# The first stage of a two-layer encoder trunk: constant matmuls ahead of it, another order of its splits, small vectors on GpSimd's queue

## The chip, the cores and the metric

The kernel runs on one core of a Trainium2 chip. The metric is the device time of one execution in microseconds (us). Three executions of the kernel before took 936.38, 937.65 and 938.26 us; their median, 937.65 us, is the time that the change is compared with. Engine names: PE is TensorE (PEld its weight loads), DVE is VectorE, ACT is ScalarE, POOL is GpSimd, SP is SyncE, which here does nothing but issue DMAs.

## What is computed

Two layers of a bidirectional encoder over 256 tokens of width 1024, all in fp32. The part that matters here is the beginning of a layer:

```
h    = rms_norm(x, g_mix)
proj = h @ w_in            # w_in: 1024 x 5792, columns split into
c_q, c_kv, k_r, d_q, d_k, d_v, s_q, s_k, s_v, gate_logits
# latent attention (c_q 256, c_kv 128, k_r 32 wide), differential attention,
# windowed attention, three sigmoid gates; then
x = x + (sum of gate * branch output) @ w_out
x = x + (gelu(conv3(h2 @ w_ffn_gate)) * (h2 @ w_ffn_up)) @ w_ffn_down
x = x + sigmoid(rms_norm(x) @ w_ple_gate) * rms_norm(p @ w_ple_proj)
```

Besides the large weights there are some twenty small vectors per layer (norm gains, convolution taps, lambda vectors, sinks), and the token positions, from which rope tables and distances are made.

## The kernel before

**Products.** Each fp32 matrix product is made as three products of a narrower format (fp32r): both operands are split into a hi part (a copy by ACT that rounds) and a lo part (the rest, a subtraction by DVE), and `mm3` (line 342) adds hi by hi, hi by lo and lo by hi in PSUM. So each weight has to pass through ACT (line 91) and DVE (line 92) before TensorE can use it. `Stream` (line 60) does this for the weights, in units of up to 128 x 1024: `_load` issues the DMA of a unit on SP's queue, `_split` makes the two parts `whi` and `wlo`, and `get` hands the next unit to the product loop after it has loaded four units ahead and split two ahead. There are four buffers each for raw, hi and lo units, so the load of unit 4 waits until unit 0 is split.

**The first stage.** Nothing of the trunk can start before x is transposed and scaled with the gain g_mix. x lies in four tiles (two token tiles t, two column halves h), loaded by `load_x`. `transpose_half` (line 378) takes one half: for each of two pairs kp of 128-column blocks it makes four transposes on TensorE into one PSUM bank, then for each block of the pair a hi part on ACT (line 352) and a lo part on DVE (line 353), scaled with the gain column `gm`. `gm` itself is a transpose of the small tile `mrow`, into which g_mix is loaded. Then `gemm` (line 395) for chunk A (c_q, c_kv, k_r; 416 columns) uses four units of 128 x 832, two blocks of h each: 12 products a unit, 48 in all, into two PSUM banks. `evict_A` copies them out.

**Order.** Lines 560 to 579 stand under a manual schedule: ACT, DVE, SP and PE run what is given there in the order in which it is written. POOL doesn't; its instructions, and everything outside of this block, are ordered by a list scheduler with priorities. In the block, both halves of x are transposed first; unit 0 is split after the first half and unit 1 after the second; then comes the product loop of chunk A, whose first `get` also splits unit 2, and so on. `load_gains(0)` stands in it too: 14 small DMAs on SP's queue into the tile `grows`, behind the first four weight units and ahead of unit 4. `finish_gains` (line 219) transposes `grows` on TensorE (`gT_ps`), behind the last product of chunk A and, in TensorE's order, ahead of the first gate chunk `g00`; the gains in `gT`, the rope tables and the position tables (`positions_setup`, line 269) follow from it at low priority.

**What follows.** The order of the rest of the mixer on TensorE is the string `ORDER` (line 51). The first point at which it needs small results of the first stage is `Tmk0`: transposes of the normalised latent keys `uk0*tok`, which need the statistics `L0st` of chunk A, computed in small steps on POOL (lines 542 to 550, 730, 732).

**Second layer's gains.** `load_gains(1)` is called behind the transposes for the FFN of layer 0 (line 1116). Its tile takes the buffer of `mrow`, and the scheduler put its memset at 3.9 us and its 14 DMAs between 27 and 48 us.

Of the kernel before, what the change touches and what calls it, by code (L numbers as in the profile page):

```python
# [11 lines left out]
F32 = mybir.dt.float32  # L12
# [6 lines left out]
P = 128  # L19
# [15 lines left out]
DEFER_M = 2  # L35
HI = 400
# [10 lines left out]
# The order of a layer's token mixer on the tensor engine, after the latent projections. Chunks of projection columns:  # L47
# g<branch><half> gates, b<branch><half> branch outputs, dq/dk/dv differential, sq/skv windowed q and kv (one word for
# each weight unit); uq/ukv latent expansions; T<x> transposes of x; and the stages of attention (m latent, d
# differential, w windowed): s scores, p transposed probabilities, o values, dt transposed differential output.  # L50
# [9 lines left out]
class Stream:  # L60
    """Weight units in the order of their use: loads run ahead of the splits, splits ahead of the products."""

    def __init__(self, nc, pools, ahead_load, ahead_split):
        self.nc = nc
        self.raw_pool, self.hi_pool, self.lo_pool = pools
        self.al, self.asp = ahead_load, ahead_split
        self.specs = []
        self.raw = {}
        self.split = {}
        self.nl = self.ns = self.nu = 0  # L70
        self.behind = {}  # unit: the instructions its hi and lo parts stay behind
# [46 lines left out]
def kernel(ctx: ExitStack, tc: tile.TileContext, a: dict, out: bass.AP):  # L118
# [37 lines left out]
    nc.sync.dma_start(mrow[0:8, :], a["g_mix"][0].rearrange("(j p) -> j p", p=P))  # L156
# [20 lines left out]
    def load_gains(l):  # L177
        g = {}
        rows = lay.tile([P, P], F32, tag="grows", name=f"grows{l}")
        nc.gpsimd.memset(rows, 1.0)  # L180
        q = nc.sync
        q.dma_start(rows[R_MIX:R_MIX + 8, :], a["g_mix"][l].rearrange("(j p) -> j p", p=P))
        q.dma_start(rows[R_QL:R_QL + 2, :], a["g_q_lora"][l].rearrange("(j p) -> j p", p=P))
        q.dma_start(rows[R_KL:R_KL + 1, :], a["g_kv_lora"][l].rearrange("(j p) -> j p", p=P))
        q.dma_start(rows[R_CW:R_CW + 66, :], a["conv_w"][l].rearrange("t (j p) -> (t j) p", p=P))
        q.dma_start(rows[R_CB:R_CB + 22, :], a["conv_b"][l].rearrange("(j p) -> j p", p=P))
        q.dma_start(rows[R_FFN:R_FFN + 8, :], a["g_ffn"][l].rearrange("(j p) -> j p", p=P))
        q.dma_start(rows[R_PIN:R_PIN + 8, :], a["g_ple_in"][l].rearrange("(j p) -> j p", p=P))
        q.dma_start(rows[R_DO:R_DO + 1, :], a["g_diff_out"][l].rearrange("(j p) -> j p", p=P))
        for r, nm in ((R_DQ, "g_diff_q"), (R_DK, "g_diff_k"), (R_WQ, "g_win_q"), (R_WK, "g_win_k")):  # L190
            q.dma_start(rows[r:r + 1, :].rearrange("j (d p) -> j d p", d=2),
                        a[nm][l].rearrange("(j d p) -> j d p", j=1, d=1).broadcast_to([1, 2, 64]))
        for r, nm in ((R_MQ, "g_mla_q"), (R_MK, "g_mla_k")):
            q.dma_start(rows[r:r + 1, 0:64], a[nm][l, 0:64].rearrange("(j p) -> j p", j=1))
        g["rows"] = rows
        return g
# [72 lines left out]
    def positions_setup():  # L269

# [6 lines left out]
        nc.vector.tensor_copy(pos_col, pos_col_i)  # L277
        pos_row = tmp.tile([P, S], F32, tag="p", name="pos_row")
        nc.vector.tensor_copy(pos_row, pos_row_i)
# [58 lines left out]
    def pin(ins):  # L338
        """Keeps an instruction behind what TensorE has been given so far."""
        order(ins, last_pe[0])  # L340
# [37 lines left out]
    def transpose_half(src, h, hi, lo, gcol, name, scale=None):  # L378
        res = []
        for kp in range(2):  # L380
            b = bank(f"{name}T{h}{kp}")
            bv = b.rearrange("p (a n) -> p a n", a=2)
            for i in range(2):
                c = (kp * 2 + i) * P
                for t in range(NT):
                    TR(bv[:, i, t * P:(t + 1) * P], src[t][h][:, c:c + P], ident)
            k0 = h * 4 + kp * 2
            if gcol is None:
                res.append(split(hi[:, k0:k0 + 2, :], lo[:, k0:k0 + 2, :], bv, scale))
            else:  # L390
                for i in range(2):
                    res.append(split(hi[:, k0 + i, :], lo[:, k0 + i, :], bv[:, i, :], gcol(k0 + i)))
        return res

    def gemm(name, nk, n, lhs, evict, alloc=None):
        accs = [(alloc or accbank)(f"{name}a{t}") for t in range(NT)]
        k = 0
        while k < nk:
# [3 lines left out]
            if k + per == nk:  # L402
                steps = [(i, t) for t in range(NT) for i in range(per)]
            for i, t in steps:
# [77 lines left out]
    def softmax_T(p_t, name):  # L482
        """P [q, (qt, k)] -> its transpose as a hi/lo pair [k, (kt, q)]."""
# [10 lines left out]
    # ================= one layer =================  # L494
    def layer(l):
# [12 lines left out]
        # 0,1: sums of squares; 2: mean square + eps; 3: its rsqrt; 4: half of that; 5: eps * (2)  # L508
# [20 lines left out]
        # 6,7: c_q, c_kv mean squares, +eps/rmix^2; 8: k_r mean square share; 9,10: their rsqrt;  # L529
        # 11: eps term of q heads; 12: k_r and eps term of k heads; 13: factor of k_r  # L530
# [26 lines left out]
        ag = gemm(n_ + "A", KT, 416, hT, evict_A)  # L557
        if l == 0:
            ET = mybir.EngineType
            with tc.manual_schedule(engines={ET.Activation, ET.DVE, ET.SP, ET.PE}):  # L560
# [8 lines left out]
                for h in range(2):  # L569
                    transpose_half(x, h, hTh, hTl, lambda k: gm[:, k:k + 1], n_ + "mix")  # L570
                    W.presplit(1 + h)
                next(ag)
                next(ag)
# [31 lines left out]
        @low  # L605
        def norm_heads(acc, nh, t, name, extra=None):
            """Per-head factor rmix * rsqrt(mean((rmix*q)^2) + eps) [* extra] of the raw projections."""
# [20 lines left out]
        def defer(n, key, fn):  # L628
            """Emits fn behind n more fill units (or before the transposes that need it)."""
            deferred.append([n, key, fn])  # L630
# [9 lines left out]
        def drain(accs, n, view=None, oview=None):  # L640
            """Copies a chunk's raw sums out of PSUM, so that its banks are free at once."""
# [172 lines left out]
        def pair_out(pts, vsel, dst, j, name):  # L814
            """Values of a pair of heads: the columns hold V's hi and lo parts, whose products are summed on the way out."""
# [13 lines left out]
        def scores2(q, k, jq, jk, name):  # L829
            """Scores of two heads held on the two halves of the partitions, one bank for each."""  # L830
# [426 lines left out]
```

## Time and profile before

| | us |
|---|---|
| median of three executions | 937.65 |
| lowest, highest | 936.38, 938.26 |
| span of the profiled execution | 933.5 |
| TensorE busy in it | 915.4 |
| DVE, ACT, POOL busy | 700.9, 604.3, 125.1 |

The profiled execution is known by its span, from its first to its last instruction; the times of whole executions lie 2.9 to 4.8 us above that span, which is what lies around it. A profile row names the engine, the line of the kernel, the operation, the tile written and the tiles read, and in brackets what the engine waited for just before. Rows that start with SPq are DMA issues on SP's queue; their time is that of the issue, not of the transfer. A row with x7 merges seven instructions in a row, and its second number runs from the first one's start to the last one's end. Consecutive matmuls overlap, so the spacing of their starts counts and not the length of one.

### The profile page before, as it was taken

The numbers are of one execution on the slowest core, as the hardware profiler recorded it, in microseconds if no ns is written. First come the engines' busy times: TensorE is split into PE (matmuls) and PEld (weight loads), VectorE is DVE, ScalarE is ACT, GpSimd is POOL, SyncE is SP. The second block draws the span as 40 slices with busy tenths as digits, with TensorE's granted clock in tenths as the row PEclk, the third lists the DMA queues.
The fourth block names the chain that finished last, engine by engine and source line by source line (L and its number), as shares of the span: only waits on it lengthen the run. The fifth ranks groups of instructions, "written<-read, shape, count | busy, mean of one in ns | idle before, by whom it ended". The sixth has DMA issues, their size and how long they took to land.

```text
span 933.5 us, 15007 instructions
## 1 busy us (share of the span) xinstructions
PE 915.4 (98%) x5511; PEld 803.1 (86%) x5511; DVE 700.9 (75%) x1193; ACT 604.3 (65%) x1084; POOL 125.1 (13%) x239
## 2 busy tenths in 40 slices
PE   7999999999999999999999999999999999999997
PEld 6888887788799999999888888787888999999986
DVE  4798789887688667677777887979766767767684
ACT  5878876885565455555676788688655555555472
POOL 2834111010110000000143423010001100000010
PEclk9999999999999999999999999999999999999999
DMA  6755435356646666666556555344465566656642
GB/s 195 223 173 167 140 100 164 108 164 199 185 136 203 188 183 190 185 181 198 151 159 185 160 165 163 111 138 116 143 216 158 177 185 180 196 175 194 193 150 87
DMA packets 101709, 155.97 MB, mean 167 GB/s; under 512 B 7316, under 2 KB 58372, under 8 KB 101636
## 3 DMA queue, kind: packets, MB, share of 16 engines
q1 hardware_dynamic: 101636, 155.02, 55.3%
q8 instruction: 43, 0.70, 0.3%
q14 instruction: 30, 0.25, 0.1%
HBM read 153.95 MB, written 1.05 MB: 166 GB/s over the span
## 4 chain that ended last, share of the span: by engine, by line
PE 87%; POOL 3%; issue 3%; ACT 3%; DVE 2%; DMA 1%; SPq 1%; POOLq 0%; ACTq 0%; DVEq 0%
PE L1u L327 7%; PE L0u L327 7%; PE L0g L327 7%; PE L1g L327 7%; PE L1dn L327 6%; PE L0dn L327 6%; PE L0g20a L327 1%; PE L1g20a L327 1%; PE L1dva L327 1%; PE L0dva L327 1%; PE L1dka L327 1%; PE L0dka L327 1%; PE L1g00a L327 1%; PE L0pg0a L327 1%; PE L1g21a L327 1%
## 5 line engine op out<-in xcount | busy, mean ns | idle before, releaser
L92 DVE TENSOR_TENSOR wlo<-raw,whi 128x1024 fp32r<-128x1024 f32 (+3 forms) x292 | 350.9, 1207 | 144.9 <-ACT whi L91 144.2
L91 ACT ACTIVATE whi<-raw 128x1024 fp32r<-128x1024 f32 (+3 forms) x292 | 304.0, 1045 | 201.9 <-PE L0g L327 28.5
L327 PE MATMUL L0g<-L0fTh,wlo 128*128 128x256 f32 x176 | 49.8, 283 | 0.0
L327 PE MATMUL L0u<-L0fTh,whi 128*128 128x256 f32 x176 | 49.8, 283 | 0.0
L327 PE MATMUL L0u<-L0fTl,whi 128*128 128x256 f32 x176 | 49.8, 283 | 0.0
L327 PE MATMUL L0u<-L0fTh,wlo 128*128 128x256 f32 x176 | 49.8, 283 | 0.0
L327 PE MATMUL L1g<-L1fTh,wlo 128*128 128x256 f32 x176 | 49.8, 283 | 0.0
L327 PE MATMUL L1u<-L1fTh,whi 128*128 128x256 f32 x176 | 49.8, 283 | 0.0
L327 PE MATMUL L1u<-L1fTl,whi 128*128 128x256 f32 x176 | 49.8, 283 | 0.0
L327 PE MATMUL L1u<-L1fTh,wlo 128*128 128x256 f32 x176 | 49.8, 283 | 0.0
L327 PE MATMUL L1g<-L1fTl,whi 128*128 128x256 f32 x176 | 49.8, 283 | 0.0
L327 PE MATMUL L0g<-L0fTl,whi 128*128 128x256 f32 x176 | 49.8, 283 | 0.0
L327 PE MATMUL L0g<-L0fTh,whi 128*128 128x256 f32 x176 | 49.8, 283 | 0.0
L327 PE MATMUL L1g<-L1fTh,whi 128*128 128x256 f32 x176 | 49.8, 283 | 0.0
L327 PEld LDWEIGHTS L0g<-L0fTl,whi 128*128 128x128 f32 x176 | 33.8, 192 | 0.4
L327 PEld LDWEIGHTS L0g<-L0fTh,whi 128*128 128x128 f32 x176 | 33.7, 192 | 0.4
L327 PEld LDWEIGHTS L1g<-L1fTl,whi 128*128 128x128 f32 x176 | 33.7, 192 | 0.4
L327 PEld LDWEIGHTS L1g<-L1fTh,whi 128*128 128x128 f32 x176 | 33.8, 192 | 0.4
L327 PEld LDWEIGHTS L0u<-L0fTh,whi 128*128 128x128 f32 x176 | 33.8, 192 | 0.0
L327 PEld LDWEIGHTS L0u<-L0fTl,whi 128*128 128x128 f32 x176 | 33.8, 192 | 0.0
L327 PEld LDWEIGHTS L0u<-L0fTh,wlo 128*128 128x128 f32 x176 | 33.8, 192 | 0.0
L327 PEld LDWEIGHTS L1u<-L1fTh,whi 128*128 128x128 f32 x176 | 33.8, 192 | 0.0
(1732 smaller groups left out, 2653.8 us busy)
## 6 DMA issues: line engine op xcount, KB each, us to landing
raw<-in_w_in_dram SPq DMA_DIRECT2D x84, 512.0 KB
raw<-in_w_ffn_gate_dram SPq DMA_DIRECT2D x44, 512.0 KB
raw<-in_w_ffn_up_dram SPq DMA_DIRECT2D x44, 512.0 KB
raw<-in_w_ffn_down_dram SPq DMA_DIRECT2D x44, 512.0 KB
raw<-in_w_branch_dram SPq DMA_DIRECT2D x24, 512.0 KB
raw<-in_w_out_dram SPq DMA_DIRECT2D x16, 512.0 KB
raw<-in_w_ple_gate_dram SPq DMA_DIRECT2D x16, 512.0 KB
raw<-in_w_in_dram SPq DMA_DIRECT2D x8, 416.0 KB
```

The lines of the kernel that those rows point to most:

```text
L91: ih = self.nc.scalar.activation(hi[:, :m], raw[:, :m], AF.Copy)
L92: il = self.nc.vector.tensor_tensor(lo[:, :m], raw[:, :m], hi[:, :m].bitcast(F32), op=ALU.subtract)
L327: last_pe[0] = nc.tensor.matmul(*args, **kw)
```

## The change

Nine matmuls of a constant tile with itself stand at the head of the program. The DMA of g_mix for `mrow` goes to ACT's queue. The 14 DMAs of the first layer's gains go to GpSimd's queue. In the first stage, each unit's split stands between the transposed pairs of blocks instead of behind a half, the products of unit 0 stand before the transposes of the second half, and they are made in another order: all those that need the hi part of the weights first. The two conversions of the positions, and the memset of the second layer's gain tile, are pinned behind the last instruction that TensorE has been given at that point. The other lines of the diff remove comments.

```diff
+WARM = 9
...
+    busy = wlo.tile([P, 1024], F32R, tag="wlo", name="busy")
+    nc.gpsimd.memset(busy[:, :512].bitcast(F32), 1.0)
+    busy_ps = pacc.tile([P, 512], F32, tag="acc", name="busy_ps")
+    for _ in range(WARM):
+        nc.tensor.matmul(busy_ps, busy[:, :P], busy[:, :512], start=True, stop=True)
     ident = const.tile([P, P], F32, name="ident")
...
-    nc.sync.dma_start(mrow[0:8, :], a["g_mix"][0].rearrange("(j p) -> j p", p=P))
+    nc.scalar.dma_start(mrow[0:8, :], a["g_mix"][0].rearrange("(j p) -> j p", p=P))
...
-        nc.gpsimd.memset(rows, 1.0)
-        q = nc.sync
+        ms = nc.gpsimd.memset(rows, 1.0)
+        if l:
+            pin(ms)
+        q = nc.sync if l else nc.gpsimd
...
-        nc.vector.tensor_copy(pos_col, pos_col_i)
+        pin(nc.vector.tensor_copy(pos_col, pos_col_i))
...
-        nc.vector.tensor_copy(pos_row, pos_row_i)
+        pin(nc.vector.tensor_copy(pos_row, pos_row_i))
...
-    def transpose_half(src, h, hi, lo, gcol, name, scale=None):
+    def transpose_half(src, h, hi, lo, gcol, name, scale=None, between=None):
         res = []
         for kp in range(2):
+            if kp and between is not None:
+                between()
...
-    def gemm(name, nk, n, lhs, evict, alloc=None):
+    def gemm(name, nk, n, lhs, evict, alloc=None, lead=False):
...
+            if lead and k == 0:
+                for i, t in steps:
+                    xh, xl = lhs(i, t)
+                    MM(accs[t][:, :n], xh, hi[:, i, :], start=i == 0, stop=False)
+                    MM(accs[t][:, :n], xl, hi[:, i, :], start=False, stop=False)
+                for i, t in steps:
+                    MM(accs[t][:, :n], lhs(i, t)[0], lo[:, i, :], start=False, stop=False)
+                steps = []
...
-        ag = gemm(n_ + "A", KT, 416, hT, evict_A)
+        ag = gemm(n_ + "A", KT, 416, hT, evict_A, lead=l == 0)
...
-                for h in range(2):
-                    transpose_half(x, h, hTh, hTl, lambda k: gm[:, k:k + 1], n_ + "mix")
-                    W.presplit(1 + h)
+                ahead, W.asp = W.asp, 0
+                transpose_half(x, 0, hTh, hTl, lambda k: gm[:, k:k + 1], n_ + "mix", between=lambda: W.presplit(1))
                 next(ag)
+                W.presplit(2)
+                transpose_half(x, 1, hTh, hTl, lambda k: gm[:, k:k + 1], n_ + "mix", between=lambda: W.presplit(3))
+                W.asp = ahead
                 next(ag)
```

## Rows read from the trace of the kernel before

**Rows 1.** Waits of TensorE, whole span: who for whom, total us, times, longest.
```profile
PE gmix_ps L330 <- DMA mrow<-in_g_mix_dram: 3.4, 1, 3.4
...
PE L0mk0b L330 <- DVE L0uk00tok L796: 1.0, 1, 1.0
```
**Rows 2.** TensorE in order of time: start us, length us, what, wait before.
```profile
5.15 1.75 PE L330 MATMUL L0mixT<-ident,x 128*128 128x128 f32 x7 [1.13 <-DMA x<-in_x_dram]
...
8.55 1.75 PE L330 MATMUL L0mixT<-ident,x 128*128 128x128 f32 x7 [0.16 <-DMA x<-in_x_dram]
...
12.80 0.55 PE L327 MATMUL L0Aa<-whi,L0hTh 128*128 128x416 f32 x1
...
13.15 0.43 PE L327 MATMUL L0Aa<-wlo,L0hTh 128*128 128x416 f32 x1
...
15.37 0.35 PE L327 MATMUL L0Aa<-whi,L0hTl 128*128 128x416 f32 x1
...
21.79 0.27 PE L330 MATMUL gT_ps<-ident,grows 128*128 128x128 f32 x1
21.82 0.48 PE L327 MATMUL L0g00a<-whi,L0hTh 128*128 128x512 f32 x1
22.69 0.50 PE L327 MATMUL L0g00a<-wlo,L0hTh 128*128 128x512 f32 x1 [0.39 <-DVE wlo L92]
```
**Rows 3.** ACT in order of time, first stage, same columns.
```profile
6.09 0.47 ACT L352 ACTIVATE L0hTh<-L0mixT,gmix 128x256 fp32r<-128x256 f32 x1 [3.88 <-PE L0mixT L330]
...
8.53 0.47 ACT L352 ACTIVATE L0hTh<-L0mixT,gmix 128x256 fp32r<-128x256 f32 x1 [0.58 <-DVE L0hTl L353]
8.91 0.89 ACT L91 ACTIVATE whi<-raw 128x832 fp32r<-128x832 f32 x1
...
13.07 2.46 ACT L91 ACTIVATE whi<-raw 128x832 fp32r<-128x832 f32 x3
...
19.10 1.06 ACT L91 ACTIVATE whi<-raw 128x1024 fp32r<-128x1024 f32 x1 [2.34 <-DMA raw<-in_w_in_dram]
...
25.00 1.28 ACT L304 ACT_TABLE_LOAD   x1
```
**Rows 4.** DVE in order of time, first stage, same columns.
```profile
9.83 1.02 DVE L92 TENSOR_TENSOR wlo<-raw,whi 128x832 fp32r<-128x832 f32 x1 [0.30 <-ACT whi L91]
10.77 0.48 DVE L353 SCALAR_TENSOR_TENSOR L0hTl<-L0mixT,gmix,L0hTh 128x256 fp32r<-128x256 f32 x1
...
13.99 2.90 DVE L92 TENSOR_TENSOR wlo<-raw,whi 128x832 fp32r<-128x832 f32 x3 [0.30 <-ACT whi L91]
...
20.12 0.17 DVE L277 CAST pos_col<-pos_col_i 128x2 f32<-128x2 int32 x1 [3.23 <-DMA pos_col_i<-in_positions_dram]
```
**Rows 5.** DMA issues of SP's queue in order of time, same columns.
```profile
1.17 0.36 SPq L156 DMA_DIRECT2D mrow<-in_g_mix_dram  x1
...
7.20 0.22 SPq L184 DMA_DIRECT2D grows<-in_g_kv_lora_dram  x1
...
15.33 0.39 SPq L80 DMA_DIRECT2D raw<-in_w_in_dram  x1
```
**Rows 6.** POOL in order of time: a memset, one step twice, a power.
```profile
1.96 0.20 POOL L180 MEMSET grows<- 128x128 f32 x1
...
16.87 0.30 POOL L513 TENSOR_SCALAR L0st<-L0st 128x1 f32<-128x1 f32 x1 [12.80 <-ACT L0mixj L512]
...
21.48 1.34 POOL L513 TENSOR_SCALAR L0st<-L0st 128x1 f32<-128x1 f32 x1 [3.06 <-ACT L0mixj L512]
...
41.91 1.05 POOL L732 TENSOR_TENSOR L0uk00ri<-L0uk00ms,mhalf 128x4 f32<-128x4 f32 x1
```
**Rows 7.** Waits of SP's queue from 205 to 262 us.
```profile
SPq L80 <- DVE wlo L92: 40.8, 16, 5.5
```
**Rows 8.** Stretches at the end: busy us of PE, PEld, DVE, ACT, POOL, granted clock, DMA.
```profile
928.00:930.00 2.00, 0.26 (x2) 0.00 (x0) 1.93 (x4) 0.69 (x1) 0.00 (x0) 1.00 0.02 8
930.00:931.00 1.00, 0.00 (x0) 0.00 (x0) 0.44 (x1) 0.00 (x0) 0.00 (x0) 1.00 0.65 246
```

## The prediction

> **What bounds the kernel now.** I read the page first: TensorE is busy for 915.4 of 933.5 us, so over the whole span only its waits and its start can give anything. Then the list of TensorE's waits: 3.4 us at the start for the gain g_mix, and behind the first stage 1.0 us at `Tmk0` [rows 1]. Then TensorE, ACT and DVE in order of time up to 25 us. Three things are to be seen. The products of chunk A run 0.35 us apart up to 13.15 us, and later 0.19: from 15.37 to 21.79 lie 34 of them [rows 2]. 416 columns in 0.35 us is the lower level of TensorE's clock (1.2 GHz), in 0.19 about the upper (2.4 GHz); the column of the granted clock says 1.00 in all of this time, so here only the spacing tells it. Second, up to 15 us TensorE waits for ACT and DVE: the first hi part starts at 6.09 [rows 3], the last three lo parts of weights run from 13.99 to 16.89 [rows 4], and from 15.37 on the products follow each other without a gap. So what ends the first stage is the split of unit 1, the first of those three, at 15 us and the products behind it. Third, the second product of `g00` starts 0.87 us behind the first instead of 0.23 (0.19 x 512/416), since unit 4 came late [rows 2]: ACT waited 2.34 us for its load [rows 3], and SP issued that only at 15.33, behind 14 small loads [rows 5].
>
> **The constant matmuls.** POOL's fill of 512 columns costs at most 4 x 0.20 = 0.8 us [rows 6], likelier 0.5, and goes first; mrow's memset, done before 1.17 [rows 5], moves behind it. TensorE starts at 1.3 to 1.5. A product of 512 columns at the lower level is 0.35 x 512/416 = 0.43 us, nine of them 3.85: they end at 5.1 to 5.3 (earlier if the clock rises on the way). The cover is the load of x, whose second tile let the transposes start at 5.15 [rows 2]; without it they would cost up to 0.4, as SP is rid of mrow's issue and that tile may land 0.4 sooner. So their own cost is 0 to 0.2.
>
> **mrow on ACT's queue.** It was issued at 1.17 [rows 5] and used at 3.4 [rows 1], 2.2 us later. Ahead of ACT's first table load it is issued by 1.7, behind it by 2.5; it lands at 3.9 to 4.7, hidden under the constant matmuls either way. The table load it may delay isn't needed before the first hi part.
>
> **The new order of splits.** The first hi part came 0.50 behind the start of the last of its four transposes, 0.22 apart (5.15 + 2 x 0.22 = 5.59, to 6.09) [rows 2, 3]. Now g_mix's transpose and four of x follow at 5.1 to 5.3: the first hi part starts at T0 = 5.9 (upper level) to 6.5 (lower); before 6.09. From there a chain runs between ACT and DVE, in steps that rows 3 and 4 show: a lo part follows its hi part 0.5 later, the bank's second hi part waits for the end of the first lo part, 0.5 after its start (0.48 long at 10.77), the weight's hi part follows 0.38 behind that (8.53 to 8.91), its lo part 0.92 later (9.83), and DVE reaches the next lo part of x 0.94 later (10.77). The first weight's hi part starts at T0 + 0.5 + 0.5 + 0.4 = T0 + 1.4 = 7.3 to 7.9; its load had landed by 7.20, when it released an issue of SP's queue [rows 5]. A round is 0.92 + 0.94 + 0.5 + 0.38 = 2.75 us, so the fourth weight's hi part starts at T0 + 9.7 and its lo part is there 0.92 + 1.0 later, at T0 + 11.6 = 17.5 to 18.1. That is later than the 16.89 of before, but now only 11 products at 0.19 stand behind it: gT's transpose comes at 19.6 to 20.2 instead of 21.79. **Gain 1.6 to 2.2 us**, if the clock is up by then.
>
> **SP's queue without the 14 loads.** Unit 4 can be loaded as soon as unit 0 is split, at T0 + 1.4 + 1.9 = 9.2 to 9.8 instead of 15.33; at 3.8 us for its landing (15.33 to 19.10) it is there at 13.5. ACT reaches it behind two sums of squares (before, it was done with the weights at 13.07 + 2.46 = 15.5 and with these at 19.10 - 2.34 = 16.8 [rows 3]), at about T0 + 11.9; its lo part is ready 2.3 later, at 20.1 to 20.7, about when g00's second product wants it. **The 0.64 us shrink to 0 to 0.1.**
>
> **What is late next.** With the gains of both parts TensorE is 2.1 to 2.8 us ahead at g00. It has to stay so at `Tmk0`, where it waited already [rows 1] for a chain ACT, POOL, DVE. That chain passes the sine's table load at 25.00, which stood behind the eviction of chunk A [rows 3], now some 2.4 earlier. The pinned conversion of positions started at 20.12 and waited for its load before [rows 4]; now it waits for gT's transpose, at about the same 20. DVE's small steps behind it have until 25.00 + 1.28 - 2.4 = 23.9, when the sine itself can start now; that leaves them nearly 4 us. The pin queues only low-priority table work behind it. So I take the wait at `Tmk0` as unchanged; if the chain doesn't follow, up to 2.4 of the gain is lost there.
>
> **The 14 loads on POOL's queue.** Here the trace has no row: no DMA is issued by POOL. The nearest below is SP's issue, 0.22 [rows 5]; above, POOL's slowest step, 1.34 for one that takes 0.30 when nothing else runs [rows 6]. I take 1.05, POOL's power on 128x4, its own longer work. They start at about 1.96 + 0.5 = 2.5 [rows 6]; 14 x 1.05 ends them at 17.2, and with 2.2 for the landing gT's transpose can go at 19.4: just ahead of the 19.6 to 20.2 where it is due. It is hidden by the first stage up to 1.07 to 1.11 each. POOL's next step, the mix statistics at 16.87, isn't due before 17.5 now. At 0.22 nothing changes; at 1.34 the transpose goes at 23.5 and TensorE, which takes it ahead of g00, waits 3.6.
> In the Trainium skill, "DMA: Bandwidth & Descriptors" (Latency and other measured facts) gives about 1 µs to the first byte for a DMA issued by GpSimd; an estimate from that page is 14 us for the 14, which would hide as well.
>
> **The second layer's loads and pins.** 14 issues of at most 0.4, some 5 us of SP's time, move from 27 to 48 us, where TensorE waits for no load, to the FFN's start. There SP itself waits 40.8 of 57 us for buffers [rows 7], and units are loaded four ahead. Cost 0; without that cover up to 5 us.
>
> **Sum.** Gain 1.6 to 2.2, and 0.5 to 0.6, less 0 to 0.2: 1.9 to 2.8, middle 2.4. The profiled span of 933.5 becomes 931.1; with the 4.15 us that lie between it and the median of 937.65, **935.2**.
>
> **Rivals.**
> *The clock doesn't hold (0.14).* For it: the rise in before came only after 4.6 us of nearly unbroken work (8.55 to 13.15 [rows 2]), transposes included; nine products and the transposes make about 5, and then TensorE has nothing for 1.5 to 2.5 us until the first weight. Against it: at the end of the program TensorE worked for 0.26 us behind 928, and the granted clock was still 1.00 up to 931, over 2.5 us without work [rows 8]. At the lower level the 12 leading products take 12 x 0.35 from about 8.5, the second half's transposes follow at 12.7 and the next hi part at 14 instead of 11.1: 2.7 lost, of which 2.4 was the gain. Time 937.7 to 938.2, and the change doesn't do what its matmuls are for.
> *Part of it is lost (0.20).* POOL's loads at 1.12 to 1.25 each, or a chain to `Tmk0` that follows by half: gain 0.3 to 1.8, time 935.9 to 937.4.
> *POOL's queue is the new bound (0.18), slower.* Place: gT's transpose in front of g00. From 1.27 each on the gain is gone (14 x 1.27 + 4.7 = 22.5); at 1.34 the time is 937.65 - 2.4 + 3.6 = 938.9. If POOL is also shut out during DVE's four weight splits (4 x 0.97), 942.7. For it: the step of 1.34 us at 21.48 lies beside a DVE split [rows 6]. Against it: the first weight split on DVE comes at 8.2 or later, when five of the loads are issued.
> The Trainium skill has this as a rule: "SBUF — State Buffer" (the "DVE blocks DMA" box) says that GpSimd cannot write the descriptors of its DMAs while VectorE holds their shared port in certain modes. The slow step agrees with a blocked port; whether a split also blocks the writing of descriptors no row shows.
>
> **How the numbers follow.** Forecast 0.48, the three rivals 0.52. Beyond 940.0 lies half of the last rival, 0.09; below 933.4 (all gains at their upper ends and the wait at `Tmk0` gone as well) 0.07. So the range is 933.4 to 940.0; the forecast's own is 934.8 to 935.8. A measurement here tells apart about 0.2%, 1.9 us: forecast faster, 0.48; the first two rivals mostly the same, 0.34; slower 0.18.
>
> **What would show it.** Products of chunk A 0.19 apart from the first one on; the four splits of weights some 2.75 us apart; gT's transpose at about 20 without a wait for a load; g00's first two products 0.23 apart; POOL's issues near 1 us. Wrong would be 0.35 between the leading products, or TensorE waiting for `grows`.

## The result

The kernel after the change takes 941.33 us (median of five executions, 940.90 to 941.69) against 936.38 us of the kernel before in executions beside it (935.07 to 938.26): 1.0056 times as long, 95% interval 1.0044 to 1.0067. It is 5.0 us **slower**, where 935.2 was predicted; the range ended at 940.0.

The profiled execution of the kernel after took 941.69 us, with a span of 939.9; that of the kernel before had 933.5. The 6.4 us between these spans are more than the 5.0 between the medians: in all profiled executions here the time lies 1.7 to 1.9 us above the span (not 2.9 to 4.8, which compared the span of one execution with the times of others), so that of the kernel before took some 935.3, less than its median. Where the two part is read from the start of the first TensorE instruction on some tiles (us, from the view by tile):

| kernel | `gT_ps` | `L0cT` | `L0ukv0a` | `L0mk0b` (Tmk0) | `L0mq0b` (Tmq0) | `L0dqb` | `L0dkb` | `L1g00a` | `L1pleT` |
|---|---|---|---|---|---|---|---|---|---|
| before | 21.8 | 28.0 | 36.9 | 47.0 | 51.0 | 81.3 | 93.2 | 476.4 | 903.2 |
| after | 21.9 | 27.5 | 36.4 | 49.8 | 55.4 | 85.8 | 99.3 | 482.8 | 909.6 |

The stage that was changed ends where it did. Up to the latent expansion `ukv0` the kernel is 0.5 us ahead. Then it falls behind in three places: 3.3 us up to Tmk0, 1.6 up to Tmq0, 1.6 between `dqb` and `dkb`. Behind 100 us it loses only 0.3 more: the second layer's 14 loads, which were moved to the FFN, cost next to nothing, as predicted.

**The first stage.** TensorE in the kernel after, in order of time (start us, length us, what, wait before):

```profile
5.52 1.48 PE L338 MATMUL L0mixT<-ident,x 128*128 128x128 f32 x8
8.94 0.46 PE L335 MATMUL L0Aa<-whi,L0hTh 128*128 128x416 f32 x1 [1.94 <-ACT whi L92]
9.24 0.36 PE L335 MATMUL L0Aa<-whi,L0hTl 128*128 128x416 f32 x1
9.44 0.35 PE L335 MATMUL L0Aa<-whi,L0hTh 128*128 128x416 f32 x1
...
10.12 0.55 PE L335 MATMUL L0Aa<-whi,L0hTl 128*128 128x416 f32 x1
10.47 0.55 PE L335 MATMUL L0Aa<-whi,L0hTh 128*128 128x416 f32 x1
...
21.95 0.48 PE L335 MATMUL L0g00a<-whi,L0hTh 128*128 128x512 f32 x1
22.27 0.40 PE L335 MATMUL L0g00a<-wlo,L0hTh 128*128 128x512 f32 x1
```

TensorE has nothing for 1.94 us behind the first eight transposes. From the second on, the first products come some 0.2 apart; from 10.12 on they are 0.35 apart. The windows of the same kernel say it outright (start and end, length, PE busy and count, granted clock, DMA share, GB/s):

```profile
9.00:11.00 2.00, 2.00 (x8) 0.71 0.97 324
11.00:13.00 2.00, 2.00 (x9) 0.50 0.92 269
...
50.00:52.00 2.00, 1.84 (x10) 0.70 0.81 244
52.00:54.00 2.00, 2.00 (x6) 0.50 0.05 18
```

0.50 is the lower of the clock's two levels, 1.2 GHz. It fell once in the first stage, after the 1.94 us without work, and a second time behind Tmk0. ScalarE, in order of time, shows what the first fall costs:

```profile
6.60 0.47 ACT L360 ACTIVATE L0hTh<-L0mixT,gmix 128x256 fp32r<-128x256 f32 x1 [2.90 <-PE L0mixT L338]
...
8.00 0.89 ACT L92 ACTIVATE whi<-raw 128x832 fp32r<-128x832 f32 x1
...
10.75 0.89 ACT L92 ACTIVATE whi<-raw 128x832 fp32r<-128x832 f32 x1
13.53 0.48 ACT L360 ACTIVATE L0hTh<-L0mixT,gmix 128x256 fp32r<-128x256 f32 x1 [1.90 <-PE L0mixT L338]
...
14.94 0.89 ACT L92 ACTIVATE whi<-raw 128x832 fp32r<-128x832 f32 x1
...
32.24 1.28 ACT L312 ACT_TABLE_LOAD   x1
33.54 0.23 ACT L312 ACTIVATE sinT<-r0.0_369 128x32 f32<-128x32 f32 x1
33.78 1.28 ACT L990 ACT_TABLE_LOAD   x1
...
36.52 1.28 ACT L312 ACT_TABLE_LOAD   x1
37.81 0.23 ACT L312 ACTIVATE cosT<-r0.25_379 128x32 f32<-128x32 f32 x1
38.06 1.28 ACT L990 ACT_TABLE_LOAD   x1
```

The second weight split follows the first by 2.75 us, as predicted; the third follows the second by 4.19, because ScalarE stood 1.90 us for transposes that came late. That is where 1.4 us of the gain of the new order went; the rest went mostly ahead of it, for the first hi part came at 6.60, where 5.9 to 6.5 was predicted.

**Behind it.** The last six of these rows are the second finding. Before, the sine's table load stood at 25.00 [rows 3], with the cosine right behind the sine. Now the sine comes at 33.54, the cosine at 37.81, and each has a table load in front of it and one behind it, where ScalarE goes back to the gate: four loads of 1.28 us in 7.1 us, in the middle of the weight splits. The longest waits of TensorE between 30 and 60 us (who for whom, total us, times, longest):

```profile
PE L0mk0b L338 <- DVE L0uk00tok L816: 2.0, 1, 2.0
PE L0uq0a L335 <- DVE wlo L93: 1.1, 1, 1.1
PE L0g01a L335 <- DVE wlo L93: 0.8, 1, 0.8
```

Before, there was 1.0 at Tmk0 alone [rows 1]. So two late splits and a later Tmk0, and then the products at the lower level behind it: from Tmk0 to Tmq0 the table has 5.6 us after and 4.0 before, which is the second place of 1.6 us. VectorE, which makes these splits, was held up by its own queue:

```profile
36.71 0.18 DVE L444 TENSOR_TENSOR L0kr<-L0araw,rpk 128x16 f32<-128x16 f32 x1 [2.40 <-POOL rpk L267]
...
38.10 0.94 DVE L93 TENSOR_TENSOR wlo<-raw,whi 128x768 fp32r<-128x768 f32 x1
...
85.61 0.68 DVE L631 TENSOR_REDUCE L0dq1ss<-L0dq1sq 128x8 f32<-128x512 f32 x1
```

The rope of the key part `k_r` waits for the rope tables `rpk`, which GpSimd makes of sine and cosine, and splits of weights queue behind it. The last row is the third place: a sum of squares of the differential q, done in the kernel before at 72.67, ahead of three weight splits, now comes after them at 85.61, and TensorE waits 1.27 us for what follows from it at `dqb`.

### The profile page after: what moved, and what is told of

The parts are those of the page before. It is cut to its first block, busy times and chain, and to the rows that moved or that the text cites. A ratio compares the mean times of both kernels' runs of the same rounds, so it can differ in the third digit from the quotient of the medians.

```text
span 939.9 us, 15028 instructions
## 1 busy us (share of the span) xinstructions
PE 920.2 (98%) x5520; PEld 806.2 (86%) x5520; DVE 700.9 (75%) x1193; ACT 607.3 (65%) x1086; POOL 133.7 (14%) x254
## 3 DMA queue, kind: packets, MB, share of 16 engines
HBM read 153.95 MB, written 1.05 MB: 165 GB/s over the span
## 4 chain that ended last, share of the span: by engine, by line
PE 87%; ACT 3%; POOL 3%; DVE 3%; issue 3%; DMA 1%; SPq 0%; POOLq 0%; ACTq 0%; DVEq 0%
PE L0u L335 7%; PE L1u L335 7%; PE L1g L335 7%; PE L0g L335 7%; PE L0dn L335 6%; PE L1dn L335 6%; PE L1g20a L335 1%; PE L0g20a L335 1%; PE L1dva L335 1%; PE L1g00a L335 1%; PE L1dka L335 1%; PE L0pg0a L335 1%; PE L1g21a L335 1%; PE L1pg0a L335 1%; PE L1sqa L335 1%
## 5 line engine op out<-in xcount | busy, mean ns | idle before, releaser
L335 PE MATMUL L0g<-L0fTh,wlo 128*128 128x256 f32 x176 | 49.8, 283 | 0.0
L335 PE MATMUL L0u<-L0fTh,whi 128*128 128x256 f32 x176 | 49.8, 283 | 0.0
L335 PE MATMUL L0u<-L0fTl,whi 128*128 128x256 f32 x176 | 49.8, 283 | 0.0
L335 PE MATMUL L0u<-L0fTh,wlo 128*128 128x256 f32 x176 | 49.8, 283 | 0.0
L335 PE MATMUL L1g<-L1fTh,wlo 128*128 128x256 f32 x176 | 49.8, 283 | 0.0
L335 PE MATMUL L1u<-L1fTh,whi 128*128 128x256 f32 x176 | 49.8, 283 | 0.0
L335 PE MATMUL L1u<-L1fTl,whi 128*128 128x256 f32 x176 | 49.8, 283 | 0.0
L335 PE MATMUL L1u<-L1fTh,wlo 128*128 128x256 f32 x176 | 49.8, 283 | 0.0
L335 PE MATMUL L0g<-L0fTl,whi 128*128 128x256 f32 x176 | 49.8, 283 | 0.0
L335 PE MATMUL L1g<-L1fTl,whi 128*128 128x256 f32 x176 | 49.8, 283 | 0.0
L335 PE MATMUL L0g<-L0fTh,whi 128*128 128x256 f32 x176 | 49.8, 283 | 0.0
L335 PE MATMUL L1g<-L1fTh,whi 128*128 128x256 f32 x176 | 49.8, 283 | 0.0
```

Source lines behind the costliest of these rows:

```text
L335: last_pe[0] = nc.tensor.matmul(*args, **kw)
```

## The experiments

The kernel before took 935.7 to 936.0 us (medians) beside each group of runs; ratios below are to it, with a 95% interval. The changed kernel wasn't run again beside them, and its own kernel before took 936.38, so a difference to its 941.33 is known to about 1 us. "Pins" are the two dependencies that the change puts on the conversions of the positions.

### What lost the time: e1 to e4

**e1: one sine.** Sine and cosine as one activation over a joint tile.

```diff
-        for dst, shift in ((sinT, 0.0), (cosT, 0.25)):
+        for i, shift in enumerate((0.0, 0.25)):
...
-            pin(nc.scalar.activation(dst, r, AF.Sin))
+        pin(nc.scalar.activation(both, rr, AF.Sin))
```

> The changed kernel, with sine and cosine of the position tables in one activation over a joint tile (64 columns instead of twice 32), so that ScalarE loads its tables twice behind the transposes of the latents instead of four times. Table theory: the two further table loads (1.28 us each) and what they make late (two weight splits, the k chain in front of Tmk0, the products at the lower clock behind that wait) are most of the loss: the wait at Tmk0 is back near 1 us, 937.0 to 938.5 us. Rival (first stage: the clock lost in the gap behind the transposes is the whole loss): ScalarE's tables lie beside other work, 941.3 us, no change. Rival (the positions come late, not the tables: the converted positions are there only at 22.4 us): Tmk0 moves by less than 0.5 us, 940.5 to 941.3 us.

938.36 us, ratio 1.0020 (1.0010 to 1.0031): 3.0 us less than the changed kernel. Two table loads are left, at 32.22 and 33.79, and the sine is as late as it was. Tmk0 comes at 48.8. VectorE and then TensorE of e1, in order of time:

```profile
37.29 0.23 DVE L443 TENSOR_TENSOR L0kr<-L0araw,rpk 128x32 f32<-128x32 f32 x1 [2.91 <-POOL rpk L265]
...
38.73 0.97 DVE L93 TENSOR_TENSOR wlo<-raw,whi 128x768 fp32r<-128x768 f32 x1
```
```profile
39.75 0.45 PE L336 MATMUL L0uq0a<-wlo,L0cTh 128*128 128x384 f32 x1 [1.85 <-DVE wlo L93]
...
40.80 0.53 PE L336 MATMUL L0uq0a<-whi,L0cTl 128*128 128x384 f32 x1
41.12 0.53 PE L336 MATMUL L0uq0a<-whi,L0cTh 128*128 128x384 f32 x1
```

With the table loads halved, the late sine shows by itself: VectorE stands 2.91 us at the rope, the split behind it is late, TensorE waits 1.85 us, and its next products run at the lower level (0.32 apart, in the kernel before 0.17 to 0.18). So both theories of the expectation hold a part; the table loads alone aren't the whole loss. Tmk0 comes 1.0 us earlier than in the changed kernel, TensorE doesn't wait there, and from there to Tmq0 it takes 3.8 us instead of 5.6.

**e2: no pins on the positions.**

```diff
-        pin(nc.vector.tensor_copy(pos_col, pos_col_i))
+        nc.vector.tensor_copy(pos_col, pos_col_i)
```

(and the same for `pos_row`)

> The changed kernel without the two pins that keep the conversion of the positions behind the transpose of the gains. The sine can then go early (behind the third split of the plan behind chunk A), but sine and cosine still stand apart on ScalarE: four table loads (sine, gate, cosine, exponential). Table theory: most of the loss stays, 939.5 to 941.3 us. Rival (late positions): the k chain is back at its old place, Tmk0 waits 1 us, 936.5 to 938 us. Rival (first stage): 941.3 us, or more, since VectorE does small position work between the first splits again.

943.16 us, ratio 1.0075 (1.0062 to 1.0088): **slower still**, for which only the last theory left room. VectorE of e2:

```profile
12.28 0.17 DVE L285 CAST pos_col<-pos_col_i 128x2 f32<-128x2 int32 x1 [4.68 <-DMA pos_col_i<-in_positions_dram]
```

Without a pin the list scheduler puts the conversion between the first two lo parts of x (7.12 and 12.72), where it waits 4.68 us for its own load; chunk A ends 3.7 us later (`gT_ps` at 25.6). The table loads are four here too. So the first stage needs a pin; the question is where it stands.

**e3: the kernel before with the two pins and nothing else.**

```diff
-        nc.vector.tensor_copy(pos_col, pos_col_i)
+        pin(nc.vector.tensor_copy(pos_col, pos_col_i))
```

(and the same for `pos_row`)

> The kernel before with only the two pins of the position conversions added; loads, order of the first splits and transposes as before. ScalarE then has four table loads between 23 and 40 us instead of two. Table theory, and the late positions too: the loss of 4 us and more at Tmk0 and behind comes with the pins alone, 939 to 941 us. Rival (first stage, or the moved loads): no more than 0.3 us from 936.4 us.

941.95 us, ratio 1.0066 (1.0054 to 1.0079). The pins alone cost the kernel before 6.2 us, 1 us more than the upper end expected, with loads, order of splits and queues untouched. ScalarE of e3 shows the pattern of the changed kernel around the two gates; the sine's own load is at 28.69:

```profile
36.28 1.28 ACT L970 ACT_TABLE_LOAD   x1
...
38.27 1.28 ACT L304 ACT_TABLE_LOAD   x1
39.56 0.23 ACT L304 ACTIVATE cosT<-r0.25_367 128x32 f32<-128x32 f32 x1
39.81 1.28 ACT L970 ACT_TABLE_LOAD   x1
```

**e4: the gap filled.** Nine more constant matmuls behind the first eight transposes.

```diff
                 transpose_half(x, 0, hTh, hTl, lambda k: gm[:, k:k + 1], n_ + "mix", between=lambda: W.presplit(1))
+                for _ in range(9):
+                    MM(busy_ps, busy[:, :P], busy[:, :512], start=True, stop=True)
                 next(ag)
```

> The changed kernel with nine more constant matmuls (128x512) behind the first eight transposes, in the 1.94 us in which TensorE waited for the first weight split. Clock theory: the products of the first half run at the higher rate to their end (about 0.11 apart instead of 0.35 between 10.1 and 12.5 us), the second half's parts come 1.5 to 2 us earlier, and chunk A ends near 20 us; what of it reaches the end is 0.5 to 2 us, since the split of the fourth unit and the chain to Tmk0 come next: 939.3 to 940.8 us. Rival (weight splits on ScalarE and VectorE set the pace of this stage whatever the clock): chunk A ends at 21.9 us as before, 941.3 us.

939.49 us, ratio 1.0036 (1.0023 to 1.0048): 1.8 us less than the changed kernel. The windows of e4:

```profile
9.00:11.00 2.00, 2.00 (x12) 1.00 0.94 329
11.00:13.00 2.00, 1.72 (x13) 1.00 0.89 261
...
50.00:52.00 2.00, 2.00 (x13) 1.00 0.79 248
```

The granted clock stays at 1.00 where it was 0.71 and 0.50, and chunk A ends at 20.8. That the gap brought the clock down is shown by this: the same products, faster for useless work ahead of them (0.19 apart; the 0.11 of the expectation was wrong). But of the 1.1 us at chunk A only 0.3 are left at Tmk0 (49.5 against 49.8). The rest of the gain comes behind it: the granted clock stays at 1.00 behind the wait of 2.0 us there, last row, and Tmq0 follows Tmk0 by 4.0 us instead of 5.6.

### The pin's place and the number of activations: e5 and e6

**e5** pins the conversion of `pos_col` behind the products of the second unit (that of `pos_row` stays pinned where it was); **e6** is e5 with the one sine of e1.

```diff
                 next(ag)
+                at.append(last_pe[0])
                 mix_stats(0)
...
-        pin(nc.vector.tensor_copy(pos_col, pos_col_i))
+        order(nc.vector.tensor_copy(pos_col, pos_col_i), at[0])
```

> The changed kernel with the conversion of the positions pinned behind the products of the second weight unit (some 17 us) instead of behind the transpose of the gains (21.8 us). The sine then stands on ScalarE behind the third weight split after chunk A, near 25 us, instead of behind the transposes of the latents at 33.5 us; sine and cosine still stand apart, with four table loads. VectorE's two sums of squares of the differential q stand side by side again. Theory of the late sine (VectorE's queue blocked by the rope of k, which waits for the tables): the cosine is still late, since it stands between two gates, so the wait at Tmk0 stays at 1.5 us or more, but the wait at dqb (1.3 us) goes: 939 to 940.5 us. Rival (the pins do their harm by being pins, whatever they stay behind): 941.3 us. Rival (only the sine matters): 936 to 937.5 us.

> As the mid pin, and sine and cosine in one activation as well: the tables are there near 25 us, ScalarE loads its tables twice, VectorE's rope of k comes ahead of the splits that it held up. Everything behind the transpose of the gains then runs as in the kernel before, and the first stage as in the changed kernel: 0.5 us ahead of the kernel before at the transposes of the latents (27.5 against 28.0). Theory: 935.0 to 936.2 us against 935.7 to 936.4 of the kernel before, 5 us less than the changed kernel. Rival (loads on GpSimd's queue, or their place among SyncE's loads, carry part of the loss): 937.5 us or more.

| median us | pin behind gT (sine at 33.5) | pin behind unit 1 (sine at 25.5 to 25.9) |
|---|---|---|
| sine and cosine apart (4 table loads) | 941.33 (the change) | 938.09 (e5; 1.0027, 1.0017 to 1.0038) |
| one activation (2 table loads) | 938.36 (e1) | 936.27 (e6; 1.0004, 0.9995 to 1.0013) |

Each of the two faults costs 1.8 to 3.2 us, and with both mended the loss is gone: e6 can't be told from the kernel before. e5 gained more than its theory had (939 to 940.5). The two gains overlap: with either fault mended the products between Tmk0 and Tmq0 no longer run at the lower level, 4.0 us in e5 and 3.8 in e1 instead of 5.6. The third place goes with the pin: in e5 and e6 `dkb` follows `dqb` by 11.9 and 12.0 us, in the changed kernel, e1, e3 and e4 by 13.5, before by 11.9. So the loads on GpSimd's queue carry no loss that can be told (they were not run by themselves), and what the change does in the first stage is worth nothing that can be told as it stands.

### Why the first stage gives nothing: e7 to e16

All of these but e10 stand on e6. **e7** adds seven constant matmuls in the gap. **e8** goes back to the old order (both groups of transposes of a half, then one weight split; the products of unit 0 in their old order too), with the first constant matmuls and the moved loads kept.

```diff
-            if lead and k == 0:
+            if False:
...
-                transpose_half(x, 0, hTh, hTl, lambda k: gm[:, k:k + 1], n_ + "mix", between=lambda: W.presplit(1))
...
+                for h in range(2):
+                    transpose_half(x, h, hTh, hTl, lambda k: gm[:, k:k + 1], n_ + "mix")
+                    W.presplit(1 + h)
+                next(ag)
```

> The kernel with the mid pin and one sine, and seven constant matmuls (128x512) in the gap behind the first eight transposes, so that TensorE is busy until the first weight split is there. Clock theory: the granted clock stays 1.00 from 7 to 22 us (0.71 and 0.50 in 9 to 13 us without them), chunk A ends 1.1 to 1.5 us earlier, as it did with nine of them, and with the stall behind it gone all of that reaches the end: 933.8 to 935.0 us. Rival (the next thing late is a weight load or the chain of k to Tmk0, which starts from ScalarE's evictions): 935.0 to 936.0 us.

> The kernel with the mid pin and one sine, but the transposes and the first weight splits in the order of the kernel before (both groups of transposes of a half, then one split), while the constant matmuls and the loads on GpSimd's and ScalarE's queues stay. What the new order alone is worth is the difference to the kernel with the mid pin and one sine. By the sum of the prediction the new order gains 1.6 to 2.2 us, so this kernel would be that much slower. Clock theory: the new order's gain is given back in its gap, so this kernel ends within 0.7 us of it, 935.0 to 936.9 us.

e7 935.99 us (0.9996, 0.9987 to 1.0005); e8 934.88 us (0.9988, 0.9979 to 0.9996). In e7 `cT` comes at 26.2 instead of 27.5 of e6, and its median is only 0.3 us less, which can't be told. Waits of TensorE behind 22 us, and windows, of e6 and then of e7:

```profile
PE L0mk0b L341 <- DVE L0uk00tok L820: 2.3, 1, 2.3
...
48.00:50.00 2.00, 1.84 (x13) 1.00 0.82 225
```
```profile
PE L0mk0b L341 <- DVE L0uk00tok L822: 2.7, 1, 2.7
...
48.00:50.00 2.00, 2.00 (x7) 0.50 0.54 203
```

The longer wait at Tmk0 takes only 0.3 of the 1.3 us: e7 is there at 46.8, e6 at 47.8. The rest goes behind it, where the clock of e7 fell and that of e6 did not: Tmq0 comes at 52.4 in e7 and at 51.8 in e6. The other executions of e7 agree: the two whose mean granted clock was 1.000 took 934.58 and 934.74 us, the nine at 0.997 or 0.998 took 935.66 to 936.72. The old order came out 1.4 us ahead of the new one, against the 1.6 to 2.2 us of the prediction.

**e9 to e12: twelve buffers instead of six for the small vectors**, since VectorE waited 1.31 us for GpSimd to free one in front of the k tokens: e9 in e7, e10 in the kernel before, e11 in e8, e12 in e6.

```diff
-    sm = pool("sm", 6)
+    sm = pool("sm", 12)
```

> The kernel with the mid pin, one sine and seven constant matmuls in the gap, and 12 buffers instead of 6 for the small vectors, so that VectorE's second sum of squares of the latent q no longer waits 1.31 us for GpSimd to free a buffer, with the k tokens that Tmk0 needs behind it. Theory (the first stage's gain was swallowed by the wait at Tmk0, 2.7 us with the filled gap): the k tokens are ready some 1.3 to 2.3 us earlier, TensorE waits 0.4 to 1.4 us there, and the clock does not fall behind it: 932.5 to 934.3 us. Rival (GpSimd's own chain to the k factors sets Tmk0): no change, 935.5 to 936.2 us.

> The kernel before with 12 buffers instead of 6 for the small vectors and nothing else. Theory: its wait of 1.0 us at Tmk0 goes, the rest is as it was: 934.6 to 935.3 us against 936.0. Rival (GpSimd's chain sets Tmk0): 936.0 us.

> The kernel with the mid pin, one sine and the old order of transposes and splits, with the constant matmuls and the moved loads, and 12 buffers for the small vectors. It stands 0.7 us ahead of the kernel before at the transposes of the latents; with the wait at Tmk0 (1.8 us) down by 1.3 or more: 933.0 to 934.0 us. Rival: 934.9 us as with 6 buffers.

> The kernel with the mid pin, one sine and the new order, no constant matmuls in the gap, and 12 buffers for the small vectors. If the new order is worth nothing by itself, since the clock falls in its gap, this stands where the old order with 12 buffers stands or up to 0.5 us behind it, 933.2 to 934.5 us, and the filled gap is 1 us or more ahead of both. If the order is worth 1.6 us in itself and only the wait at Tmk0 hid it, this is 1.4 to 1.6 us ahead of the old order, 931.6 to 932.4 us.

e9 935.12 (0.9986, 0.9977 to 0.9995), e10 936.87 (1.0004, 0.9995 to 1.0013), e11 935.33 (0.9991, 0.9982 to 1.0000), e12 936.98 us (1.0009, 1.0000 to 1.0018). Against e7, the kernel before, e8 and e6 that is 0.9 less, 0.9, 0.5 and 0.7 more, where the theory had each of them faster by 0.7 us or more and e9 by 1.7: it fell. The waits of e12 and VectorE of e9 say why:

```profile
PE L0mq0b L341 <- DVE L0uq01tok L448: 1.2, 1, 1.2
PE L0mk0b L341 <- DVE L0uk00tok L820: 1.2, 1, 1.2
PE L0mk0b L341 <- DVE L0uk01tok L820: 1.2, 1, 1.2
```

```profile
44.90 0.42 DVE L821 TENSOR_TENSOR L0uk01tok<-L0ukv0a,L0uk01ri 128x256 f32<-128x256 f32 x1 [0.92 <-POOL L0uk01ri L758]
```

The tokens then wait for GpSimd's powers one by one, and one wait became three. By this it is the chain on GpSimd that has to start earlier.

**e13 to e16: the exponential beside the sine.** e6 and e8 also differ in where ScalarE goes back to the gate's tables: in e8 the exponential of lambda stands right behind the sine and takes the load there (25.15); in e6 the first gate does (34.19), in front of the weight splits that lead to Tmk0. e13 is e6 with the exponential put behind the sine; e14 adds seven constant matmuls in the gap; e15 is e14 with twelve buffers; e16 is e13 with one constant matmul instead of nine ahead of the transposes.

```diff
-        nc.scalar.activation(sc[:, 6:8], sc[:, 4:6], AF.Exp)
+        with tc.high_priority(offset=LOW if l == 0 else 0):
+            ex = nc.scalar.activation(sc[:, 6:8], sc[:, 4:6], AF.Exp)
+        if l == 0:
+            order(ex, sine[0])
```

> The kernel with the mid pin, one sine and the new order, and the exponential for lambda right behind the sine, so that ScalarE loads both tables near 25 us, ahead of the latents' sums of squares, as it does with the old order. If the table load in front of the gates (1.28 us in the chain of weight splits to Tmk0) was what set the new order behind the old one, this comes to 934.7 to 935.4 us, level with the old order. If the order itself costs, it stays at 936.0 to 936.5 us.

> The same with seven constant matmuls in the gap behind the first eight transposes. Clock theory: 1.3 us earlier at the transposes of the latents. If GpSimd's chain to Tmk0 and Tmq0 starts earlier with it, 0.7 to 1.3 us reach the end: 933.6 to 934.6 us. Rival (the chain starts from table loads and weight loads that don't move): within 0.3 us of the same without them.

> The same with 12 buffers for the small vectors as well. If buffers hold back part of the gain at Tmk0, 0.3 to 1 us less than with 6: 933.0 to 934.0 us. If GpSimd's chain alone sets it, the wait moves to Tmq0 and the time is that with 6 buffers.

> The kernel of the exponential by the sine with one constant matmul ahead of the first transpose instead of nine. Clock theory: the first eight transposes then run at the lower rate throughout, the gap behind them is shorter, and the products of the first half run at the lower rate as they do with nine: 0 to 0.5 us later. If the nine matmuls had made the clock of the first half, 1.5 us later.

e13 935.41 (0.9994, 0.9986 to 1.0003), **e14 933.62** (0.9970, 0.9959 to 0.9980), e15 934.01 (0.9979, 0.9970 to 0.9988), e16 935.85 us (0.9997, 0.9988 to 1.0006). The first hi part and the table loads of e14, its TensorE at the end of chunk A, and its waits between 30 and 60 us:

```profile
5.66 0.47 ACT L368 ACTIVATE L0hTh<-L0mixT,gmix 128x256 fp32r<-128x256 f32 x1 [1.93 <-PE L0mixT L346]
...
22.37 1.28 ACT L319 ACT_TABLE_LOAD   x1
...
25.47 1.28 ACT L252 ACT_TABLE_LOAD   x1
```
```profile
8.06 0.45 PE L343 MATMUL L0Aa<-whi,L0hTh 128*128 128x416 f32 x1 [0.39 <-ACT whi L92]
...
19.68 0.27 PE L346 MATMUL gT_ps<-ident,grows 128*128 128x128 f32 x1
```
```profile
PE L0g01a L343 <- DVE wlo L93: 0.6, 1, 0.6
...
PE L0mk0b L346 <- DVE L0uk00tok L827: 0.2, 1, 0.2
```

Four things follow. The new order alone against the old one (e13 against e8) makes no difference that can be told: what it gains, its gap gives back. The filled gap is worth 1.8 us (e14 against e13); whether it would be worth as much with the old order wasn't tried. It is worth that only with the chain to Tmk0 out of the way: in e7, which differs from e14 in the exponential's place alone, the same seven matmuls gain 0.3, and the two stand 2.4 us apart. In the traces GpSimd's power for the first k tokens starts 14.2 us behind `cT` in e14 and 15.5 in e7; with no long wait left at Tmk0 the clock stays at 1.00 behind it, and the mean granted clock of all eight executions of e14 is 0.999. And eight of the nine constant matmuls at the start are worth 0.4 us, which can't be told from nothing (e16 against e13). e14 is 2.4 us faster than the kernel before and 7.7 faster than the changed one; more buffers (e15) add nothing.

## Why the prediction was wrong

**What is late next: this step failed.** It saw that the pin moves the conversion to about the same time (20 us; it was 22.4), and took the pin for harmless, since "the pin queues only low-priority table work behind it". That work is the sine and the rope tables, and the table work stands in front of weight splits in two in-order queues: on ScalarE the sine, which brings two table loads with it, on VectorE the rope, which waits for the tables. The prediction gave VectorE's steps until 23.9, when the sine could start; they were interleaved with splits of higher priority, the sine's done at 27.0 and the cosine's at 29.1, and the sine then found its place only at 33.5. It also priced the loss at no more than 2.4, the gain in front; e3 shows 6.2 for the pins by themselves. Part of the loss is the clock once more, which the prediction followed only in the first stage: in the changed kernel 1.6 us are lost at the lower level between Tmk0 and Tmq0, and in e3 the granted clock is 0.50 from 46 to 48 us. The missing rival was this one: a low-priority step that comes late costs nothing by itself, but everything behind it in its queue.

**The new order of splits: the term of 1.6 to 2.2 us was lost, most of it to the clock.** T0 was 6.60 (5.9 to 6.5 predicted), the first weight split 8.00 (7.3 to 7.9), a round 2.75 as worked out, except for the one round that the clock stretched to 4.19. The rival "the clock doesn't hold" was right in its place: it put the second half's hi part at 14, and it came at 13.53. Its size was less than the rival's 2.7, since the first products still ran at the upper level: the third split came 1.4 us late. I gave it 0.14, mostly for a row at the end of the program where the granted clock stayed at 1.00 over 2.5 us without work [rows 8]; that row didn't carry over. With the gap filled `gT_ps` came 14.0 us behind the first hi part (e7: 20.6 and 6.62; e14: 19.7 and 5.66), where 13.7 was predicted, against 15.3 in the changed kernel; so the steps of the term were right to 0.3 us for a clock that holds. That e14 lies inside the predicted 19.6 to 20.2 is luck in part: its profiled execution started 0.9 us earlier than that of the changed kernel, and 14.0 us from the latter's start would end at 20.6, a gain of 1.2.

**SP's queue without the 14 loads: right.** Unit 4 was issued at 9.97 (9.2 to 9.8 predicted) and `g00`'s second product came 0.32 us behind its first instead of 0.87 [rows 2]. These 0.5 us are the whole lead at `cT`.

**The 14 loads on GpSimd's queue: hidden, as predicted, but the price was wrong.** GpSimd in the kernel after:

```profile
3.12 0.79 POOL L190 DMA_DIRECT2D grows<-in_g_mix_dram  x1
...
9.45 0.53 POOL L199 DMA_DIRECT2D grows<-in_g_diff_q_dram  x1 [1.91 <-DMA grows<-in_g_mix_dram]
...
12.09 0.49 POOL L202 DMA_DIRECT2D grows<-in_g_mla_k_dram  x1
```

An issue takes 0.53 us, half of the 1.05 taken; the queue is done at 12.6 instead of 17.2. The rival with this queue as the bound, which held all of my chance for "slower", was wrong. No issue was stretched by VectorE: the one at 9.45 lies beside a weight split (8.92 to 9.94) and takes 0.53 like the others. The Trainium skill's rule in "SBUF — State Buffer" (the "DVE blocks DMA" box) is for a VectorE instruction in a 2-port performance mode; no run here shows that the split runs in one, so the trace doesn't test the rule. The 2.2 us taken for the landing were too few: the ninth load waited for the first, issued at 3.12, until 9.45. The 1 µs that the Trainium skill's "DMA: Bandwidth & Descriptors" (Latency and other measured facts) gives for a GpSimd DMA is the time to its first byte, and says little of such a landing.

**mrow: right; the constant matmuls: a little too cheap.** TensorE started at 1.30, ScalarE issued mrow's load at 1.57 ahead of its table load, and the wait for g_mix was gone. The nine matmuls ended at the late end of what was predicted (g_mix's transpose at 5.31), the transposes of x started at 5.52 instead of 5.15, and the first hi part came 0.5 later than before [rows 3], where 0 to 0.2 was taken. In other profiled executions with the same nine it came between 5.66 (e14) and 6.62 (e7).

**The sum.** Of the 1.9 to 2.8 us of gain 0.5 came true; the pins then took some 5. The 4.15 us that the sum adds to the span aren't what lies around it, which is 1.7 to 1.9: it took the span of one execution and the median of others, so its starting point was 1.3 us above the median measured beside the change. What stays open is the remainder of the chain to Tmk0: which of GpSimd's steps would have to move for e14 to gain more was not tried.

## What to carry to other kernels

Before an instruction is pinned or moved, follow what depends on it to the in-order queues in which its consumers stand, and price what is queued behind those consumers; low priority says when an instruction is given, not what it holds up. On ScalarE, activations that share a table belong next to one another, or in one activation over a joint tile, and a change of tables belongs ahead of the stage whose splits it would break. A gain in front is worth only what the next wait, and the clock behind it, let through: here 1.3 us at `cT` were worth 0.3 at the end while the wait at Tmk0 grew with them and the clock fell behind it, and with the chain to Tmk0 started earlier the same matmuls were worth 1.8.

## What was not expected of the hardware

- In the kernel after, TensorE's clock fell behind the gap of 1.94 us in the first stage, and behind the wait of 2.0 us at Tmk0, and in e7 behind a wait of 2.7 us there. Behind waits of 2.0 us (e4) and 2.3 us (e6) at the same place it stayed at 1.00. What tells these cases apart wasn't settled.
- In the kernel after, a DMA issue on GpSimd takes 0.49 to 0.56 us (0.79 for the first one), and the ninth one waits for the first, until 6.3 us after that one's issue. Whether the chip or the program sets the number eight no run shows.
- A load of ScalarE's tables takes 1.28 us each time, and in the kernel after it was paid twice for one sine and twice for one cosine of 128 x 32.
